# Grouped-query attention: the order of scores, turns and values on TensorE

## The chip, the cores and the metric

The kernel runs on one core of a Trainium2 chip. The metric is the device time of one execution in microseconds; before the change it is 1549.0 us, the median of 3 runs (1548.19 to 1549.32). The core has five engines that run side by side and wait for each other through semaphores: TensorE (PE in the profile, its weight loads PEld), VectorE (DVE), ScalarE (ACT), GpSimd (POOL) and SyncE (SP), which issues most transfers. Each engine works through its own instructions in one fixed order.

## The reference

One step of a two-layer trunk with 640 tokens: 512 latent tokens and 128 prompt tokens, model width 1024, 16 heads of 64. Layer 0 mixes tokens with neighbourhood attention, layer 1 with grouped-query attention, and each is followed by a gated ConvFFN. All of it is fp32. The change is in the attention of layer 1, which computes for the latent tokens

```python
qs, ks_ = axial_rope(qs), axial_rope(ks_)                 # after per-head RMS norms
k_all = jnp.concatenate([ks_, cache_gqa_k[:, i]], axis=1) # 512 latent + 128 cached keys
v_all = jnp.concatenate([vs, cache_gqa_v[:, i]], axis=1)
s = jnp.einsum('bqkgd,bskd->bkgqs', qi, k_all) * HEAD_DIM ** -0.5
p = jax.nn.softmax(s, axis=-1)
o = jnp.einsum('bkgqs,bskd->bqkgd', p, v_all)             # 16 query heads, 4 key heads
```

and then `xs + g * rmsnorm(o @ w_o)`. The prompt's own attention, 128 queries on 128 keys, is small beside it.

## The kernel before

The layers run one after the other. In layer 1 the products for keys, values and queries come first, then the attention loop, then the output projection `y` (`Mix`, L724) and the ConvFFN. The attention loop stands at L1838 and takes 34 steps.

Its work is cut into 32 **units**, `Unit` (L1663). A unit is one head and one half of the latent queries (256 of 512). Units come in the order: half 0 of heads 0 and 1, half 1 of heads 0 and 1, half 0 of heads 2 and 3, and so on. Two units that follow each other, an even and an odd one, form a **pair**. A unit goes through three stages:

- **Scores** (L1680), in two batches of 128 queries, called `s0` and `s1`. A batch is four matmuls on TensorE into a tile of two PSUM banks (`d0` for `s0`, `d1` for `s1`, one buffer each, so a batch waits until the batch before in the same tile has been read). DVE takes the minimum (L1691; the queries carry a minus sign, so it stands for the maximum), ACT the Exp with its sum (L1692), DVE the reciprocal (L1694), POOL multiplies by it (L1695).
- **Turns** (L1697). The 640 probabilities of each batch must be transposed: ten turns of 128 x 128 per unit, in three groups of 4, 4 and 2. Each group takes one PSUM bank `tp` from a list (`Banks`, L77), and ACT (L1706) or DVE (L1708) copies it to SBUF as `pk`. ACT copies the first group of every unit and the third of even units, DVE the others. The bank goes back to the end of the list; whoever gets it next waits for that copy.
- **Values** (L1713), for both units of a pair together: ten matmuls into the bank `po`. The bank is taken at half 0 and given back only after half 1 of the same two heads, when ACT casts it (L1725) and DVE subtracts (L1726).

Of the eight PSUM banks four belong to `d0` and `d1` in the loop (L1764 to L1766), and four stand in the list for `tp`, `po` and the prompt's steps.

What runs in which order is written out by hand in `GORDER` (L70): one list for even steps, one for odd ones. At step `u`, `s0` and `s1` are the scores of unit `u + 2`, `t0` to `t2` the three turn groups of unit `u`, `l0` to `l2` those of unit `u - 1`, `v` the values of the units `u - 2` and `u - 1`, and `p` one step of the prompt's attention (from step 6 on, until they are used up). TensorE runs its instructions in just that order (L110). On ACT, DVE and POOL a scheduler chooses the order when the program is built, from the same program.

At the loop's end the four banks of the scores are handed to the list (L1857), the output projection starts at step 30 with the weights `wh` and `wl`, which ACT and DVE split out of `wr` (L178, L180), and the turns of the last pair run between its products.

Of the kernel before, what the change touches and what calls it, by code (L numbers as in the profile page):

```python
# [66 lines left out]
DLEAD = 3  # L67
DPRE = (8, 10, 12, 14)
KP = (2, 2, 2, 2, 1)
GORDER = ("s0 p v s1 t0".split(), "s0 l1 l2 t0 s1 t1 t2".split())  # L70


def raw_ap(ap, offset, dims):
# [31 lines left out]
def hybrid_step(ctx: ExitStack, tc: tile.TileContext, A, O):  # L105
# [1707 lines left out]
    with ExitStack() as s:  # L1813
# [24 lines left out]
        for u in range(NU + 2):  # L1838
            if u + 2 < NU:
                un[u + 2] = Unit(u + 2)  # L1840
            for step in GORDER[u % 2]:
                if step == "p":
# [119 lines left out]
```

## Time and profile before

| what | value |
|---|---|
| median of 3 runs | 1549.0 us (1548.19 to 1549.32) |
| profiled execution, its own time | 1550.43 us |
| its span | 1548.6 us |
| granted TensorE clock, mean | 0.998 |
| busy: PE, PEld, DVE, ACT, POOL | 98%, 87%, 66%, 55%, 45% of the span |
| the attention loop | about 921 to 1063 us of the span |

The profile shows one execution. Its span runs from the first to the last instruction; the execution's own time is a little longer. A row of the timeline gives the start in us, the duration in us, engine, line of the kernel, operation, out<-in and the count of merged instructions; what stands in brackets is the idle time before and who ended it. TensorE's matmuls overlap, so their cost is read from one start to the next. The records of a product of fp32 values count two for each matmul. Names there leave buffer numbers out: `s` is a score tile, `gp` the probabilities, `nmg` the minimum, `rcg` the reciprocal, `tp`, `pk` and `po` as above, `gkh` and `gkl` the two parts of the keys, `gq` the queries.

### The profile page before, as it was taken

What the parts mean: (1) busy time and instruction counts of PE and PEld (TensorE: products, weight loads), DVE (VectorE), ACT (ScalarE), POOL (GpSimd) and SP (SyncE); (2) the same over time, 40 slices, a digit from 0 to 9 for tenths busy, and PEclk for the clock granted to TensorE, in tenths of its full rate; (3) what the DMA queues carried; (4) which work ended last, traced back from release to release, by engine and by line L of the source; (5) the groups of instructions that cost most, each with busy time, mean ns of one, the idle gap of its engine ahead of it and who ended that gap; (6) DMA issues with size and microseconds to landing.
All of it is one profiled execution on the core that took longest, in us unless ns stands there. A gap on an engine that the chain in (4) does not pass through costs nothing.

```text
span 1548.6 us, 26098 instructions
## 1 busy us (share of the span) xinstructions
PE 1513.5 (98%) x9709; PEld 1343.4 (87%) x9709; DVE 1022.3 (66%) x1648; ACT 854.0 (55%) x1624; POOL 702.2 (45%) x606
## 2 busy tenths in 40 slices
PE   6999999999999999999999999999999999999998
PEld 5988998888999999978887878778899999988886
DVE  4553343659877666755757877773988887786554
ACT  5664564646655555554544447763665665564443
POOL 1554564432355455525443464532235666542433
PEclk9999999999999999999999999999999999999999
DMA  9745454253565665388574421015433335447664
GB/s 324 199 123 161 121 134 116 64 189 125 176 225 182 222 190 162 111 279 272 174 238 153 131 67 44 2 34 196 153 115 114 120 110 158 132 161 251 226 220 131
DMA packets 196666, 243.99 MB, mean 158 GB/s; under 512 B 11484, under 2 KB 153020, under 8 KB 196540
## 3 DMA queue, kind: packets, MB, share of 16 engines
q1 hardware_dynamic: 186704, 235.74, 47.8%
q10 hardware_dynamic: 9836, 6.59, 2.5%
q8 instruction: 76, 1.25, 0.3%
q14 instruction: 50, 0.41, 0.1%
HBM read 214.38 MB, written 26.34 MB: 155 GB/s over the span
## 4 chain that ended last, share of the span: by engine, by line
PE 63%; DVE 5%; ACT 2%; issue 2%; POOL 2%; DMA 1%; POOLq 0%; DVEq 0%; ACTq 0%
PE ux L117 18%; PE acc L117 17%; PE uz L117 8%; PE gp L117 5%; PE uy L117 4%; PE po L117 3%; PE y L117 2%; PE s L117 2%; PE tp L120 2%; PE ada L117 1%; DMA wr<-in_ffn_w_down 1%; DVE t L1281 1%; POOL wl L180 1%; DMA wr<-in_ffn_w_up 1%; DVE wl L180 1%
## 5 line engine op out<-in xcount | busy, mean ns | idle before, releaser
L180 POOL TENSOR_TENSOR wl<-wr,wh 128x1024 fp32r<-128x1024 f32 x70 | 173.8, 2487 | 239.8 <-ACT wh L178 228.7
L1204 POOL TENSOR_TENSOR wl<-wr,wh 128x1024 fp32r<-128x1024 f32 x76 | 183.6, 2438 | 46.9 <-ACT wh L1203 43.3
L117 PE MATMUL ux<-B,wh 128*128 128x322 f32 x832 | 200.0, 311 | 0.9 <-ACT u L1258 0.9
L1281 DVE SCALAR_TENSOR_TENSOR t<-C,cw,t 128x644 f32<-128x644 f32 x176 | 156.4, 888 | 51.3 <-ACT t L1279 50.7
L178 ACT CAST wh<-wr 128x1024 fp32r<-128x1024 f32 x140 | 145.5, 1048 | 53.8 <-DMA wr<-in_ffn_w_down 41.1
L117 PE MATMUL acc<-wh,alo 128*128 128x512 f32 x440 | 172.3, 392 | 0.3 <-DVE alo L1173 0.3
L117 PE MATMUL acc<-wl,ahi 128*128 128x512 f32 x440 | 171.9, 391 | 0.5 <-POOL wl L180 0.5
L117 PE MATMUL acc<-wh,ahi 128*128 128x512 f32 x440 | 171.9, 391 | 0.0
L117 PE MATMUL uz<-B,wh 128*128 128x322 f32 x640 | 156.2, 312 | 0.9 <-ACT v L1258 0.9
L117 PEld LDWEIGHTS ux<-B,wh 128*128 128x128 f32 x832 | 143.6, 189 | 3.3 <-issue 1.2
L1173 DVE TENSOR_TENSOR alo<-ain,ahi 128x384 fp32r<-128x384 f32 (+1 forms) x88 | 81.8, 948 | 88.9 <-ACT ahi L1171 88.6
L117 PE MATMUL ux<-B,wl 128*128 128x322 f32 x416 | 129.5, 311 | 3.0 <-DVE wl L1204 3.0
L117 PE MATMUL qk<-hT,wh 128*128 128x384 f32 (+1 forms) x512 | 122.3, 315 | 0.0
L117 PEld LDWEIGHTS uz<-B,wh 128*128 128x128 f32 x640 | 110.9, 189 | 4.4 <-ACT v L1258 1.5
L1204 POOL TENSOR_TENSOR vl<-wr,vh 128x1024 fp32r<-128x1024 f32 x38 | 96.4, 2537 | 24.6 <-ACT vh L1203 24.3
L1203 ACT CAST wh<-wr 128x1024 fp32r<-128x1024 f32 x84 | 84.8, 1049 | 40.9 <-DVE wr L1227 40.6
L1279 ACT ACTIVATE t<-C,cw 128x644 f32<-128x644 f32 x88 | 78.6, 893 | 47.8 <-DVE C L1309 40.2
L180 DVE TENSOR_TENSOR wl<-wr,wh 128x1024 fp32r<-128x1024 f32 x70 | 91.4, 1315 | 19.3 <-ACT wh L178 18.7
L117 PE MATMUL uz<-B,wl 128*128 128x322 f32 x320 | 99.6, 311 | 0.3 <-POOL wl L1204 0.3
L117 PEld LDWEIGHTS acc<-wl,ahi 128*128 128x128 f32 x440 | 82.6, 188 | 18.9 <-POOL wl L180 0.9
L117 PEld LDWEIGHTS acc<-wh,alo 128*128 128x128 f32 x440 | 82.5, 188 | 18.7 <-DVE alo L1173 1.1
L117 PEld LDWEIGHTS acc<-wh,ahi 128*128 128x128 f32 x440 | 82.6, 188 | 17.7
(259 smaller groups left out, 3858.2 us busy)
## 6 DMA issues: line engine op xcount, KB each, us to landing
wr<-in_ffn_w_up SPq DMA_DIRECT2D x88, 512.0 KB
wr<-in_ffn_w_down SPq DMA_DIRECT2D x88, 512.0 KB
wr<-in_ada_w SPq DMA_DIRECT2D x72, 512.0 KB
act<-act SPq DMA_DIRECT2D x44, 321.0 KB
wr<-in_na_w_qkv SPq DMA_DIRECT2D x24, 512.0 KB
mod<-modrow SPq DMA_DIRECT2D x20, 512.0 KB
ain<-act SPq DMA_DIRECT2D x44, 192.0 KB
wf<-in_ada_w SPq DMA_DIRECT2D x16, 512.0 KB
```

The costliest lines, as they stand in the source:

```text
L117: pe(nc.tensor.matmul(*a, **k))
L120: pe(nc.tensor.transpose(*a, **k))
L178: i = nc.scalar.copy(hi, raw)
L180: j = (low or nc.vector).tensor_sub(lo, raw, f32(hi))
L1173: pin(nc.vector.tensor_sub(lo[:, 0 : c1 - c0], ain[:, 0 : c1 - c0], f32(hi[:, 0 : c1 - c0])))
L1203: nc.scalar.copy(hl[0], src)
L1204: low.tensor_sub(hl[1], src, f32(hl[0]))
L1279: nc.scalar.activation(t, taps(0), AF.Identity, bias=cw[:, 3, n : n + 1], scale=cw[:, 1, n : n + 1])
L1281: nc.vector.scalar_tensor_tensor(t, taps(d), cw[:, w, n : n + 1], t, op0=ALU.mult, op1=ALU.add)
```

## The change

The two lists are written anew. The diff is complete:

```diff
-GORDER = ("s0 p v s1 t0".split(), "s0 l1 l2 t0 s1 t1 t2".split())
+GORDER = ("s0 p v s1".split(), "s0 l0 l1 l2 t0 t1 t2 s1".split())
```

Even steps lose their turn group. Odd steps do all six groups of the pair, even unit first, between `s0` and `s1`. An even step's `s1` is now followed at once by the odd step's `s0`, and an odd step's `s1` by the even step's `s0`. Line numbers stay as they are.

The first place is TensorE in one pair in the middle of the loop, from the values of one pair to those of the next. Before:

```order
L117 MATMUL po<-pk,gvt 64x256 x10
L117 MATMUL s_11455<-gkh,gq_9265 128x320 x2
L117 MATMUL s_11455<-gkl,gq_9265 128x320 x2
L120 MATMUL tp<-ident,gp 128x128 x4
L117 MATMUL s_11475<-gkh,gq_9266 128x320 x2
L117 MATMUL s_11475<-gkl,gq_9266 128x320 x2
L120 MATMUL tp<-ident,gp 128x128 x10
L117 MATMUL s_11503<-gkh,gq_9266 128x320 x2
L117 MATMUL s_11503<-gkl,gq_9266 128x320 x2
L120 MATMUL tp<-ident,gp 128x128 x6
L117 MATMUL s_11528<-gkh,gq_9265 128x320 x2
L117 MATMUL s_11528<-gkl,gq_9265 128x320 x2
```

Now:

```order
L117 MATMUL po<-pk,gvt 64x256 x10
L117 MATMUL s_11455<-gkh,gq_9265 128x320 x2
L117 MATMUL s_11455<-gkl,gq_9265 128x320 x2
L117 MATMUL s_11468<-gkh,gq_9266 128x320 x2
L117 MATMUL s_11468<-gkl,gq_9266 128x320 x2
L120 MATMUL tp<-ident,gp 128x128 x20
L117 MATMUL s_11515<-gkh,gq_9266 128x320 x2
L117 MATMUL s_11515<-gkl,gq_9266 128x320 x2
L117 MATMUL s_11528<-gkh,gq_9265 128x320 x2
L117 MATMUL s_11528<-gkl,gq_9265 128x320 x2
L117 MATMUL po<-pk,gvt 64x256 x10
```

Twenty turns that stood in three pieces between four score batches now stand in one; the score batches stand two by two.

The second place is ACT in the same pair. `gp_11431` is the Exp of the even unit's batches (its second reads `s2_11455`), `pk_...<-tp_...` are the copies of turn groups. Before:

```order
L1692 ACTIVATE gp_11431,sug_11433<-s2_11435,nmg_11432 128x640
L1706 COPY pk_11469<-tp_11464 128x512
L1692 ACTIVATE gp_11431,sug_11433<-s2_11455,nmg_11432 128x640
L1706 COPY pk_11494<-tp_11491 128x256
L1692 ACTIVATE gp_11471,sug_11473<-s2_11475,nmg_11472 128x640
L1706 COPY pk_11501<-tp_11496 128x512
L1692 ACTIVATE gp_11471,sug_11473<-s2_11503,nmg_11472 128x640
```

Now:

```order
L1692 ACTIVATE gp_11431,sug_11433<-s2_11435,nmg_11432 128x640
L1692 ACTIVATE gp_11431,sug_11433<-s2_11455,nmg_11432 128x640
L1706 COPY pk_11482<-tp_11477 128x512
L1692 ACTIVATE gp_11464,sug_11466<-s2_11468,nmg_11465 128x640
L1706 COPY pk_11494<-tp_11491 128x256
L1706 COPY pk_11501<-tp_11496 128x512
L1692 ACTIVATE gp_11464,sug_11466<-s2_11515,nmg_11465 128x640
```

The copy of the pair's first turn group stood ahead of the Exp of `s2_11455` and now stands behind it; the next two copies stand behind the Exp of the batch after it. In this pair the bank `po` is held; in the pairs in which it has just been cast, the first copy stands ahead of both Exps.

The third place is TensorE at the loop's end, where the output projection begins. Before:

```order
L117 MATMUL s_11788<-gkh,gq_9266 128x320 x2
L117 MATMUL s_11788<-gkl,gq_9266 128x320 x2
L120 MATMUL tp<-ident,gp 128x128 x6
L117 MATMUL po<-pk,gvt 64x256 x10
L120 MATMUL tp<-ident,gp 128x128 x4
L117 MATMUL y_11855<-wh,ph_10242 128x512
L117 MATMUL y_11855<-wl,ph_10242 128x512
```

Now:

```order
L117 MATMUL s_11800<-gkh,gq_9266 128x320 x2
L117 MATMUL s_11800<-gkl,gq_9266 128x320 x2
L117 MATMUL po<-pk,gvt 64x256 x10
L117 MATMUL y_11848<-wh,ph_10242 128x512
L117 MATMUL y_11848<-wl,ph_10242 128x512
L117 MATMUL y_11848<-wh,pl_10243 128x512
```

The last scores now stand directly ahead of the values, and the four turns behind the values have moved behind the first `y` group, where sixteen turns of before have become twenty.

## The prediction

> **What bounds the kernel now.** I read the page first, then the stage of the grouped-query scores by windows, then TensorE's timeline in it. The page's first row is TensorE's; the row below it is the loop that the change edits, 924 to 1040 us.
>
> ```profile
> PE 1513.5 (98%) x9709; PEld 1343.4 (87%) x9709; DVE 1022.3 (66%) x1648; ACT 854.0 (55%) x1624; POOL 702.2 (45%) x606
> ```
> ```profile
> 924.00:1040.00 116.00, 113.23 (x875) 92.06 (x876) 86.93 (x184) 85.01 (x201) 54.51 (x72) 1.00 0.06 19
> ```
>
> In the loop the columns are the length, then busy time of PE, PEld, DVE, ACT and POOL, the clock and the DMA share. TensorE is never long idle, ACT has 85 of 116 us and DVE 87, POOL and DMA little. So TensorE's order of work sets the pace, and what it waits for is ACT and DVE handing back PSUM. One pair of units, from value product to value product, on TensorE (start, duration, engine, line):
>
> ```profile
> 1007.20 2.38 PE L117 MATMUL po<-pk,gvt 128*64 128x256 f32 x20
> 1009.51 0.56 PE L117 MATMUL s<-gkh,gq 128*128 128x320 f32 x2
> 1009.91 0.46 PE L117 MATMUL s<-gkl,gq 128*128 128x320 f32 x2
> 1010.21 0.60 PE L120 MATMUL tp<-ident,gp 128*128 128x128 f32 x4
> 1010.56 0.54 PE L117 MATMUL s<-gkh,gq 128*128 128x320 f32 x2
> 1010.94 0.46 PE L117 MATMUL s<-gkl,gq 128*128 128x320 f32 x2
> 1011.23 1.25 PE L120 MATMUL tp<-ident,gp 128*128 128x128 f32 x10
> 1012.27 0.56 PE L117 MATMUL s<-gkh,gq 128*128 128x320 f32 x2
> 1012.67 0.46 PE L117 MATMUL s<-gkl,gq 128*128 128x320 f32 x2
> 1013.08 0.87 PE L120 MATMUL tp<-ident,gp 128*128 128x128 f32 x6
> 1013.71 0.53 PE L117 MATMUL s<-gkh,gq 128*128 128x320 f32 x2
> 1014.08 0.45 PE L117 MATMUL s<-gkl,gq 128*128 128x320 f32 x2
> 1014.46 2.38 PE L117 MATMUL po<-pk,gvt 128*64 128x256 f32 x20
> ```
>
> Costs go from start to start. The values take 2.31; a score batch 0.70 after values, 0.67 after turns (1010.56 to 1011.23), 0.75 between turns and values; ten turns 1.04, so 0.105 each. The pair takes 7.26, of which 0.2 is waiting: the batch at 1012.27 holds on for 0.81 instead of 0.67, and six turns take 0.63.
>
> There are 14 such intervals between the first value product at 928.45 and the one at 1036.00. I split them by whether the burst of turns inside runs while `po` keeps a PSUM bank (half 0 of a head pair has been summed, half 1 not: 7 intervals, "held") or after `po` was copied out (7, "freed"). These windows show the sum of the held ones; of the freed ones a plain one, the last, and the sum.
>
> ```profile
> sum 51.49, PE 51.49; mean PE 7.36
> ```
> ```profile
> 1014.46:1022.16 7.70, 7.42 (x57) 1.00 0.01 2
> 1029.42:1036.00 6.58, 6.58 (x53) 1.00 0.00 1
> sum 56.06, PE 54.07; mean PE 7.72
> ```
>
> A held interval without a prompt step is 7.26, as above; five of the freed ones carry a prompt step and are longer.
>
> **What the change takes away and adds on TensorE.** Nothing is removed: per pair it stays at 16 score matmuls, 20 turns, 10 value products. Only the order differs, so the work alone is 2.31 + (0.70 + 0.59) + 20 x 0.105 + (0.67 + 0.67) = 7.04. The 0.59 is a batch behind another: four times half of the 0.29 that two matmuls take from 1010.94 to 1011.23. Before it is 7.26 - 0.2 = 7.06. Grouping the kinds buys 0.02 per pair, nothing.
>
> What the old order pays is the score tile's reuse: d0 and d1 each wait until the Exp before has read them.
>
> ```profile
> PEld s L117 <- ACT gp L1692: 6.9, 13, 1.2
> PE s L117 <- ACT gp L1692: 2.9, 7, 0.9
> ```
>
> The shortest distance there is d1, between the two batches at 1009.51 and 1012.27; the new order spaces both tiles by either values plus a batch (2.9) or the burst plus a batch (2.7). From the end of a batch to the end of its Exp I need 0.82 + 0.8 + 0.2 (rows below), about 1.9, so these waits go.
>
> **What it adds: the banks.** A burst of 20 turns is six fills of a bank: even unit 4, 4, 2, then odd unit 4, 4, 2. Four banks are in the list, three when `po` holds one. So in a held burst fill 4 needs the bank of fill 1, and 6 that of 3, both copied out by ACT. The order of ACT's rows shows that in held pairs the Exp of the first side-by-side batch is queued ahead of that first copy, and the Exp of the second ahead of the third fill's copy. ACT and DVE durations:
>
> ```profile
> 1006.93 0.80 ACT L1692 ACTIVATE gp<-s,nmg 128x640 f32<-128x640 f32 x1 [0.27 <-DVE nmg L1691]
> 1010.84 0.59 ACT L1706 COPY pk<-tp 128x512 f32<-128x512 f32 x1 [1.11 <-PE tp L120]
> 1011.33 0.81 ACT L1692 ACTIVATE gp<-s,nmg 128x640 f32<-128x640 f32 x1
> 1012.11 0.37 ACT L1706 COPY pk<-tp 128x256 f32<-128x256 f32 x1
> 1016.91 0.59 ACT L1725 CAST ph<-po 128x512 fp32r<-128x512 f32 x1
> ```
> ```profile
> 1006.07 0.82 DVE L1691 TENSOR_REDUCE nmg<-s 128x1 f32<-128x640 f32 x1 [0.46 <-PE s L117]
> 1010.41 0.82 DVE L1691 TENSOR_REDUCE nmg<-s 128x1 f32<-128x640 f32 x1 [0.48 <-PE s L117]
> 1012.33 0.69 DVE L1708 COPY pk<-tp 128x512 f32<-128x512 f32 x1
> 1013.16 0.82 DVE L1691 TENSOR_REDUCE nmg<-s 128x1 f32<-128x640 f32 x1
> 1013.90 0.15 DVE L1694 RECIPROCAL rcg<-sug 128x1 f32<-128x1 f32 x1
> 1018.41 0.68 DVE L1726 TENSOR_TENSOR pl<-po,ph 128x512 fp32r<-128x512 f32 x1
> ```
>
> A minimum starts 0.04 after the scores' end (1009.91 + 0.46 to 1010.41) and takes 0.82, though DVE goes on after 0.74 (1013.16 to 1013.90); the Exp starts 0.04 after that (1006.89 to 1006.93) and gives ACT free after 0.78 (1011.33 to 1012.11); a copy of 512 columns takes 0.59 and ACT goes on after 0.49. A bank comes back to TensorE about 0.05 after its copy (1012.33 + 0.69 to 1013.08).
>
> A held pair, from the end of the values: first batch 0 to 0.70, visible at 0.86; minimum 0.90 to 1.72; Exp 1.76, ACT free at 2.54; first copy 2.54 to 3.13; fill 4 may start at 3.18. TensorE is there at 0.70 + 0.59 + 10 x 0.105 = 2.34: it waits **0.84**. Fills 4 and 5 then end at 4.02. ACT meanwhile: second Exp 3.03 to 3.81, third copy to 4.18, so fill 6 may start at 4.23: **0.21** more. The pair is 7.04 + 1.05 = 8.09, against 7.26: +0.83. The values at 5.78 wait for nothing: fill 5's last turn is through at about 4.02 + 0.25 (the four-turn row's 0.60 less its 0.35), its copy on DVE 0.69 later, about 5.0. Seven of them: **+5.8**.
>
> A freed pair: ACT casts `po` 0.14 after the values (1016.91 less 1016.77) to 0.73, DVE subtracts from 0.77 (0.68, of which I let the next overlap 0.08 as behind the minimum), runs two minima at 0.74 each and reaches the copy of fill 2 at 2.85, done 3.54. Fill 6 needs that bank: 3.59 against 3.18, a wait of 0.41, so 7.45 where the trace has 7.70: -0.25. That holds for the one plain interval. The five with a prompt step have another bank or more ACT work ahead of the burst; the ends are -0.25 and the held pair's +0.83, and I take +0.2 each, nearer the freed row. Together **+0.7**. The last interval has one batch less: 2.31 + 1.29 + 2.10 + 0.41 + 0.75 = 6.86 against 6.58, **+0.3**.
>
> **The two ends of the loop.** At the start four turns stood in a wait and cost nothing:
>
> ```profile
> 923.20 0.60 PE L120 MATMUL tp<-ident,gp 128*128 128x128 f32 x4
> 924.74 0.56 PE L117 MATMUL s<-gkh,gq 128*128 128x320 f32 x2 [0.94 <-ACT gp L1692]
> ```
>
> They move behind that batch: **+0.4** (from 0 to 0.8, if a bank is late too). At the end, the output projection's first matmuls wait for their weights, which ACT splits only after the last Exp:
>
> ```profile
> 1036.00 2.64 PE L117 MATMUL po<-pk,gvt 128*64 128x256 f32 x20
> 1038.57 0.66 PE L120 MATMUL tp<-ident,gp 128*128 128x128 f32 x4
> 1039.50 0.50 PE L117 MATMUL y<-wl,ph 128*128 128x512 f32 x1
> ```
> ```profile
> 1037.10 3.88 ACT L178 CAST wh<-wr 128x1024 fp32r<-128x1024 f32 x4
> ```
> ```profile
> 1038.16 4.69 DVE L180 TENSOR_TENSOR wl<-wr,wh 128x1024 fp32r<-128x1024 f32 x4 [0.68 <-ACT wh L178]
> ```
>
> From these values to the first `y<-wl` it is 3.50. Between the last scores and the values stood six turns (0.63 in the pair above); in the new order the scores stand directly before the values, so 3.50 becomes 4.13: +0.63, and up to 1.1 as the last minimum queues behind two copies on DVE; I take 0.9. The four turns at 1038.57, free today, move into the later burst between the `y` groups: 0.4. Together **+1.3**. From there everything is released by these matmuls; loads of later weights start when their buffers are read, so they shift along and cover nothing.
>
> Sum: 5.8 + 0.7 + 0.3 + 0.4 + 1.3 = **+8.5 us**. The profiled run has a span of 1548.6 (1550.4 with what lies around it), 0.4 and 1.4 us from the runs' median of 1549.0, on which I put it: **1557.5 us**. Bounds: with fill 6 never late in held pairs (+0.62), freed ones all at -0.25 and the last at 0, no loss at the start and 0.6 at the end it is +3.4; with held pairs at +1.1 (the Exp 0.27 later), prompt intervals at +0.83, and 0.8, 0.5 and 2.0 for start, last interval and end, about +15.
>
> **Rivals.** *The score waits were the real price (faster).* If ACT gets to each first copy before fill 4 asks for it, held pairs fall to 7.04 (51.49 - 49.3 = 2.2 saved), six freed ones lose 0.66 each (4.0), and the ends cost 1.7: 1544.5. For it stand the 9.8 us of waits above; against it, ACT's order in held pairs. It decides where the wait at the fourth fill is under 0.2.
>
> *A wash.* If `po`'s bank does not matter, held bursts wait 0.41 like freed ones: 7.45, +0.19 each, 1.3; freed ones at -0.25 take 1.5 back, the last gives 0.3: with both ends of the loop covered 1549. Against it: the list has four banks, and a value product keeps one until half 1.
>
> *Later copies hold up the values too.* Fill 5's copy stands behind two reciprocals on DVE that wait for the Exps. If it lands 0.5 after the values are due in each of 14 intervals, 7 us come on top: 1564.5. My layout leaves 0.7 of slack.
>
> *The clock falls in the bursts.* At half clock 16 bursts of 2.10 take 34 us more: 1591. The trace has a burst of sixteen turns at the loop's end, and it ran at the full granted clock:
>
> ```profile
> 1048.90:1050.57 1.67, 1.67 (x18) 1.00 1.02 410
> ```
>
> The Trainium skill ("TensorE: Matmul & The Clock Gate", Part 4: PE-mode transpose) says that transposes do not count as busy for the clock gate, and by that rule longer bursts could let the clock drop. The row just shown does not agree; a repeated burst of twenty no run here shows yet.
>
> That the change doesn't do what it says is out: the order shows twenty turns in one row.
>
> **How the numbers follow.** Forecast 0.83, wash 0.06, faster 0.04, late values 0.06, clock 0.01. A measurement here tells about 0.2% (3.1 us) from no change. Faster is the first rival, 0.04; same is most of the wash, 0.05; slower 0.91. The range 1553.5 to 1561 runs from near the lower bound to half-way between forecast and upper bound and leaves about 2 in 10 out.
>
> **What would show it.** Right: held intervals near 8.1, with a wait of TensorE's turns on ACT's copy (L1706) of some 0.8; freed ones near 7.4 without a prompt step; waits of scores on the Exp nearly gone; 1.00 clock; `y<-wl` some 4.4 after the last values but one start. Wrong: if held intervals stay at 7.3 the bank argument falls; if the value products wait for copies, the late-values rival holds.

## The result, and the profile after

The change takes 1557.58 us, the median of 4 runs (1556.74 to 1558.56). The kernel before took 1549.09 us beside it (4 runs, 1548.19 to 1549.32). The ratio is 1.0056, with a 95% interval of 1.0044 to 1.0068: slower by 8.5 us, and by more than the 0.2% that a measurement here can tell. The profiled execution took 1557.03 us, with a span of 1554.9.

The first row of the page after:

```profile
PE 1513.8 (97%) x9709; PEld 1344.1 (86%) x9709; DVE 1026.3 (66%) x1648; ACT 850.8 (55%) x1624; POOL 702.0 (45%) x606
```

TensorE has the same work in the same number of instructions. The span is longer by what it waits. The windows of the loop after, TensorE alone, split as in the prediction: the sum of the seven held intervals, the sum of the seven freed ones, and one plain interval of each kind (from:to, length, busy time of PE with its count, granted clock, DMA share, GB/s).

```profile
sum 57.45, PE 52.54; mean PE 7.51
sum 55.44, PE 53.92; mean PE 7.70
1009.82:1017.88 8.06, 7.33 (x57) 1.00 0.00 0
1017.88:1025.36 7.48, 7.31 (x57) 1.00 0.00 0
```

The held intervals grew from 51.49 to 57.45. The freed ones did not grow: 55.44 against 56.06. Before, TensorE was busy for all of the held 51.49; now 4.9 of the 57.45 are idle.

Three rows of the view of waits after (us in total, times, longest):

```profile
PE tp L120 <- ACT pk L1706: 4.6, 7, 0.7
PE tp L120 <- DVE pk L1708: 1.8, 8, 0.5
PEld s L117 <- ACT gp L1692: 3.8, 10, 0.4
```

The row in which TensorE's score matmuls waited for the Exp (2.9 us before) has no successor, and the loads' wait on it fell from 6.9 to 3.8. New are the first two rows. Seven times a turn waits for ACT's copy, once in each held interval. Eight times one waits for DVE's copy: at the sixth fill of each freed interval, and once in the held one at 943.33, which carries other work. TensorE in one held pair, from the values of one pair to those of the next:

```profile
1025.36 2.38 PE L117 MATMUL po<-pk,gvt 128*64 128x256 f32 x20
1027.67 0.56 PE L117 MATMUL s<-gkh,gq 128*128 128x320 f32 x2
...
1028.65 0.46 PE L117 MATMUL s<-gkl,gq 128*128 128x320 f32 x2
1028.94 1.25 PE L120 MATMUL tp<-ident,gp 128*128 128x128 f32 x10
1030.93 1.40 PE L120 MATMUL tp<-ident,gp 128*128 128x128 f32 x10 [0.73 <-ACT pk L1706]
1032.08 0.54 PE L117 MATMUL s<-gkh,gq 128*128 128x320 f32 x2
...
1033.03 0.46 PE L117 MATMUL s<-gkl,gq 128*128 128x320 f32 x2
1033.42 0.87 PE L117 MATMUL po<-pk,gvt 128*64 128x256 f32 x6
```

The loop's first burst, which waits for nothing:

```profile
923.90 2.35 PE L120 MATMUL tp<-ident,gp 128*128 128x128 f32 x20
926.00 0.54 PE L117 MATMUL s<-gkh,gq 128*128 128x320 f32 x2
```

Twenty turns take 2.10 there (923.90 to 926.00). In the held pair they take 3.14 (1028.94 to 1032.08), so 1.04 of it is waiting. The burst stops after ten turns, that is, after fills 1 to 3. Inside a burst of this trace one turn starts 0.109 after the one before, so ten turns with more behind them take 1.09; from 1028.94 to 1030.93 it is 1.99. The fourth fill waits 0.90 and the second ten turns lose the other 0.14. ACT at that place:

```profile
1029.42 0.80 ACT L1692 ACTIVATE gp<-s,nmg 128x640 f32<-128x640 f32 x1 [1.66 <-DVE nmg L1691]
1030.21 0.58 ACT L1706 COPY pk<-tp 128x512 f32<-128x512 f32 x1
1030.67 0.81 ACT L1692 ACTIVATE gp<-s,nmg 128x640 f32<-128x640 f32 x1
```

The copy of fill 1 runs from 1030.21 to 1030.79, right behind the first Exp, and the fourth fill starts 0.14 after its end. The loop's last values and the first products of the output projection:

```profile
1040.24 2.72 PE L117 MATMUL po<-pk,gvt 128*64 128x256 f32 x20
...
1044.75 0.49 PE L117 MATMUL y<-wl,ph 128*128 128x512 f32 x1 [0.76 <-DVE wl L180]
```

From the values to the first `y<-wl` it is 4.51 (3.50 before).

The whole loop, from its first score matmul to its last value product, by starts:

| part of the loop (us) | before | after | difference |
|---|---|---|---|
| first score to first values | 7.05 | 7.46 | +0.41 |
| seven held intervals | 51.49 | 57.45 | +5.96 |
| five freed intervals with a prompt step | 41.78 | 41.14 | -0.64 |
| the plain freed interval | 7.70 | 7.48 | -0.22 |
| the last freed interval | 6.58 | 6.82 | +0.24 |
| values of the last pair but one to those of the last | 24.31 | 25.79 | +1.48 |
| sum | 138.91 | 146.14 | +7.23 |

### The profile page after: what moved, and what is told of

Read it like the earlier page. It is cut to its first block, busy times and chain, and to the rows that moved or that the text cites. A ratio compares the mean times of both kernels' runs of the same rounds, so it can differ in the third digit from the quotient of the medians.

```text
span 1554.9 us, 26071 instructions
## 1 busy us (share of the span) xinstructions
PE 1513.8 (97%) x9709; PEld 1344.1 (86%) x9709; DVE 1026.3 (66%) x1648; ACT 850.8 (55%) x1624; POOL 702.0 (45%) x606
## 4 chain that ended last, share of the span: by engine, by line
PE 59%; DVE 7%; issue 3%; ACT 3%; DMA 3%; POOL 2%; ACTq 0%; POOLq 0%; DVEq 0%
PE ux L117 18%; PE acc L117 15%; PE uz L117 8%; PE uy L117 4%; PE gp L117 3%; PE y L117 2%; PE po L117 2%; PE s L117 2%; PE tp L120 2%; PE ada L117 1%; DMA wr<-in_ffn_w_down 1%; DVE nmg L1691 1%; POOL wl L180 1%; DMA wr<-in_ffn_w_up 1%; DVE wl L180 1%
```

## The experiments

Two readings of the loss in held bursts stood against each other. By the first, the *order on ACT* is the cause: an Exp stands ahead of the first copy. By the second, the *number of banks* is: six fills with three banks need ACT and DVE to hand back three of them within the burst, whatever stands first. Beside them the score tiles' reuse and the two ends of the loop were priced. Each kernel was profiled; where a ratio is given, it is against the kernel before, run beside it on the same chip. Medians of before there were 1549.0 us (first four experiments, 18 runs), 1548.1 (next four, 18 runs) and 1548.64 (last four, 15 runs).

### The bank of the values given back after every pair

```diff
 # values
-        if u.hf == 0:
-            ta["po"] = bk.get("po")
+        ta["po"] = bk.get("po")
...
+        c, src = slice(256 * u.hf, 256 * u.hf + 256), ta["po"][:, 256 * u.hf : 256 * u.hf + 256]
+        nc.scalar.copy(hi[:, c], src)
+        nc.vector.tensor_sub(lo[:, c], src, f32(hi[:, c]))
+        bk.put(ta["po"])
```

ACT's cast and DVE's subtraction of 512 columns behind every second pair become 256 columns behind every pair, and every burst has four banks.

> The changed kernel, but the value products of each pair get a bank of their own and give it back at once (ACT casts and DVE subtracts 256 columns per pair instead of 512 per two pairs), so that no burst of turns runs with three banks. Bank theory: held intervals fall from 8.06 to 7.5 to 7.6 (the burst then waits only for fill 2's copy on DVE, as in the freed intervals, 7.48), the rest stays; seven held intervals give 7 x -0.5 = -3 to -4, the extra cast and subtraction take some of it back: about 1554.5 us, 0.997 to 0.999 of the changed kernel. Rival 'the number of banks does not matter, score batches side by side are slow as such': held intervals stay at 8.06 and the time at 1557.6. Rival 'later copies hold the values': no change either.

Measured: 1550.38 us (10 runs), ratio 1.0011 [1.0001, 1.0020]. The sums of held and freed intervals in the windows of this kernel, named by their places although no burst has a bank too few any more; then a plain held one and the plain freed one:

```profile
sum 52.59, PE 51.56; mean PE 7.37
sum 54.05, PE 53.26; mean PE 7.61
1007.75:1015.20 7.45, 7.25 (x57) 1.00 0.00 0
1015.20:1022.40 7.20, 7.20 (x57) 1.00 0.00 0
```

The bank takes back 4.9 of the 6.0 us that the held intervals had lost, and 1.4 come off the freed ones: the median falls by 7.2, from 1557.58. The plain held intervals are 7.20 to 7.46 (8.06 in the change), the plain freed one 7.20 (7.48).

The scheduler also chose a new order on ACT, and that has to be kept apart from the bank. In the held interval of 7.45 and in the next one ACT has the order of the change: Exp (from 1011.81), first copy (from 1012.59), the other Exp. There the fourth bank alone turns 8.06 into 7.45, although ACT and DVE also have 256 columns of `po` to read that the change does not read there; only the fifth fill still waits, 0.4, for the copy of fill 1. In the intervals of 7.20, such as the freed one shown, the first copy stands ahead of both Exps (1019.42, 1019.91, 1020.69), and no turn waits. Between the freed 7.20 and the 7.48 of the change lie this order of ACT and half as many columns of `po` to cast and subtract; the two were not tried apart.

### One bank less

```diff
         mod_row()
+        held = bk.get("held")
...
+            if u == NU - 3:
+                bk.put(held)
```

> The changed kernel with one bank of the list set aside during the loop: two instead of three banks in held bursts, three instead of four in freed ones. Bank theory: freed plain interval from 7.48 to about 8.0, as held ones are with three banks; held ones from 8.06 to about 8.5; about 14 x 0.45 = +6 us, 1564 us. Rival 'banks do not matter': 1557.6, intervals unchanged.

Measured: 1565.44 us (4 runs), ratio 1.0105 [1.0090, 1.0120]. A plain held and a plain freed interval:

```profile
1015.01:1023.63 8.62, 7.59 (x58) 1.00 0.00 0
1023.63:1031.49 7.86, 7.45 (x58) 1.00 0.01 2
```

ACT keeps the order of the change in both. With that order plain held pairs take 8.62 with two banks, 8.06 with three (the change) and 7.45 with four (the kernel above); plain freed ones 7.86 with three and 7.48 with four. So the number of banks sets the length of the burst, and in this order one bank is worth 0.4 to 0.6 us a pair.

### ACT's first copy ahead of the second Exp

```diff
-                    un[u + 2].scores(int(step[1]))
+                    if u % 4 == 2 and step == "s1":
+                        wait_exp = un[u + 2].scores(1, True)
+                    else:
+                        un[u + 2].scores(int(step[1]))
...
+                    if step == "l0" and wait_exp:
+                        wait_exp(un[u - 1].ci)
```

In held pairs the Exp of the even step's `s1`, which ran ahead of the first copy, is put behind it: with `True`, `scores` hands back its Exp, reciprocal and multiplication to be issued later, and `ci` is the copy of `l0`.

> The changed kernel with ACT's queue turned round in held pairs: the Exp of the first side-by-side batch goes behind the copy of the burst's first fill. Theory A (the prediction's wording: that Exp ahead of the first copy costs 0.84 at fill 4): that wait goes, held intervals fall from 8.06 to about 7.4, 7 x -0.65 = -4.5 us, 1553 us. Theory B (what sets the burst is all that ACT must do before the third fill's copy, two Exps and the first copy, whatever their order): fill 4 starts 0.5 sooner and fill 6 then waits that much longer; held intervals stay at 8.1 to 8.2, 1557.5 to 1558.5 us.

Measured: 1558.62 us (4 runs), ratio 1.0065 [1.0050, 1.0080]: not better than the change. The plain held interval in the windows:

```profile
1011.40:1019.62 8.22, 7.49 (x57) 1.00 0.00 0
```

TensorE's burst in one held pair, and ACT beside it:

```profile
1030.68 2.48 PE L120 MATMUL tp<-ident,gp 128*128 128x128 f32 x18
1033.78 0.44 PE L120 MATMUL tp<-ident,gp 128*128 128x128 f32 x2 [0.62 <-ACT pk L1714]
```
```profile
1031.32 0.59 ACT L1714 COPY pk<-tp 128x512 f32<-128x512 f32 x1 [1.82 <-PE tp L120]
1031.80 0.80 ACT L1694 ACTIVATE gp<-s,nmg 128x640 f32<-128x640 f32 x1
1032.58 0.79 ACT L1694 ACTIVATE gp<-s,nmg 128x640 f32<-128x640 f32 x1
1033.35 0.86 ACT L1714 COPY pk<-tp 128x256 f32<-128x256 f32 x2
```

Eighteen turns stand in one row now. The row is 2.48 long, where eighteen turns without a wait take 2.13 (at 1037.01 in the change): the fourth fill still waits 0.3 for the copy of fill 1, which ends at 1031.91, instead of 0.90. But the copy of fill 3 now stands behind both Exps, and the sixth fill waits 0.8 for it. The whole burst takes 3.29 (1030.68 to the scores at 1033.97), so 1.19 of it is waiting, against 1.04 in the change. Most of the wait has moved from fill 4 to fill 6, and it has grown. With three banks, the order of Exp and first copy alone is not the cause. With four it matters: the first experiment has 7.20 with the copy ahead and 7.45 with the Exp ahead.

### First and third copy together

```diff
 # as the kernel above, and in turns:
-            if j == 0 or j == 2 and self.b == 0:
+            if j == 0 or j == 2 and self.b == 1:
```

The copy of fill 3 goes to DVE, that of fill 6 to ACT.

> As the run with ACT's queue turned round, and the third fill's copy (256 columns, even unit) goes to DVE, the sixth fill's to ACT instead. Theory B: now neither fill 4 nor fill 6 waits for the Exps; fill 4 from about 2.4 to 2.6 after the values, fill 6 at about 3.45 for DVE's copy, so held intervals about 7.3 (7 x -0.75 = -5), freed ones +0.1 each for the extra DVE copy: about 1552.5 us. Theory A: the same as the run with the copy first, since fill 4 was all. If neither bank nor copies matter: 1557.6.

Measured: 1553.39 us (9 runs), ratio 1.0031 [1.0021, 1.0041]. The plain held interval:

```profile
1006.97:1014.36 7.39, 7.28 (x58) 1.00 0.00 0
```

Now three banks nearly do: 7.39. What is left is a wait of 0.3 at the fourth fill, for the copy of fill 1. The plain freed interval, where DVE also has the subtraction of `po`, is 7.69 instead of 7.48, twice the loss that was expected.

### The third copy alone

The one line of the kernel above, on the change.

> The changed kernel with the third fill's copy on DVE and the sixth's on ACT, the Exp left ahead of the first copy in held pairs. Theory B (fill 4 waits until 3.2 for the first copy, fill 6 then asks at about 4.0 and finds its bank copied at 3.4): only the second of the two waits goes, held intervals 7.75 to 7.9 instead of 8.06, plain freed ones about 7.7; 1556 to 1557 us. If the third copy were all that counts, held intervals would be 7.4, as with both edits.

Measured: 1556.09 us (one run). The plain held interval:

```profile
1009.89:1017.84 7.95, 7.22 (x57) 1.00 0.00 0
```

This completes a square of held intervals: neither edit 8.06, first copy early 8.22, third copy on DVE 7.95, both 7.39. Alone, the edits bring -0.16 and 0.11; together 0.67. Plain held intervals of one execution differ by 0.02 at most in these four kernels. So there is no single late copy: two fills of the burst, the fourth and the sixth, wait for ACT, and to free one lets TensorE run into the other.

### One score batch back in the burst

```diff
-GORDER = ("s0 p v s1".split(), "s0 l0 l1 l2 t0 t1 t2 s1".split())
+GORDER = ("s0 p v s1".split(), "s0 l0 l1 l2 s1 t0 t1 t2".split())
```

> The changed kernel with the odd step's last score batch put into the middle of the burst, ten turns ahead of it and ten behind. Bank theory: ACT and DVE get a batch's time (0.67) more between fill 3 and fill 4, so the turns' waits on copies go; but the batch now comes 1.6 behind the batch before it in the same score tile and waits for its Exp: 0.3 in held intervals (7.4), about 1.0 in freed ones, where that Exp stands behind the first copy (plain one 8.1). Together about 1554.5 to 1555.5. Rival 'score batches side by side are slow as such': held and freed both fall to about 7.3.

Measured: 1555.30 us (4 runs), ratio 1.0047 [1.0033, 1.0061]. Sums of held and freed intervals:

```profile
sum 53.19, PE 52.08; mean PE 7.44
sum 59.61, PE 53.96; mean PE 7.71
```

Held intervals recover 4.3 us: the batch gives the copies 0.7 us more in the middle of the burst, and in the view of waits no turn waits for a copy any more. But freed ones lose 4.2 us, to this wait on TensorE in a freed pair:

```profile
1022.50 1.25 PE L120 MATMUL tp<-ident,gp 128*128 128x128 f32 x10
1024.57 0.56 PE L117 MATMUL s<-gkh,gq 128*128 128x320 f32 x2 [0.81 <-ACT gp L1692]
```

The batch after ten turns comes before the Exp has read its tile: 2.07 from start to start, 1.03 more than ten turns take. This is the price of a score tile that is asked for again too early; the prediction said that the change removes it, and the change does.

### The old lists at the end of the loop

```diff
-            for step in GORDER[u % 2]:
+            for step in (GORDER if u < NU - 4 else GOLD)[u % 2]:
```

`GOLD` holds the two lists of before.

> The changed kernel, with the old lists for the loop's last four units and its end alone. The prediction's end term: from the last values to the first y<-wl back from 4.51 to 3.5 (here six turns stand between the last scores and the values again), and the four turns stand in that wait again: last value product to last value product 25.79 to about 24.3; 1.4 us in all. If the end term were something else (the weights' transfer, the banks handed over), these distances would stay.

Measured: 1558.28 us (one run), no better than the change in total. TensorE at the loop's end (the lines are one further down here):

```profile
1042.32 2.50 PE L118 MATMUL po<-pk,gvt 128*64 128x256 f32 x20
...
1045.77 0.50 PE L118 MATMUL y<-wl,ph 128*128 128x512 f32 x1
```

From the values to `y<-wl` it is 3.45, and the last part of the loop takes 24.29 where the change has 25.79: the end term is 1.5 us, and it comes from the order of the last steps. The total hides it, since in this execution the loop's start took 9.07 instead of 7.46, at a lower clock (last section).

### Both cures, with the new lists and with the old

Two kernels take the bank given back after every pair and the third copy on DVE: one with the new lists and the old end, one with the old lists throughout.

> New lists with the bank of the values given back after every pair, the third fill's copy on DVE and the sixth's on ACT, and the old lists at the loop's end. Theory B: no burst with three banks, no third copy behind two Exps: held 7.1 to 7.2 without a prompt step, freed plain 7.1, end as before: about 1546.5 us, 2 to 3 us under the kernel before. If only the order of the lists decided, it would stay near 1556.

> The kernel before with its old lists, and the same two edits of banks and copies: the bank of the values given back after every pair, third fill's copy on DVE, sixth's on ACT. Theory B: the gain of those two is not the new order's own; intervals near 7.2, freed plain 7.2 instead of 7.70, about 1546 us, the same as the new lists with these edits. If the new order is worth something once the banks are free, this one is slower than the new lists with the edits by 1 us or more.

Measured beside each other: new lists 1546.56 us (11 runs), ratio 0.9994 [0.9986, 1.0003]; old lists **1543.94 us** (8 runs), ratio 0.9973 [0.9962, 0.9984]. Sums of held and freed intervals, new lists and then old lists:

```profile
sum 51.92, PE 51.49; mean PE 7.36
sum 53.73, PE 53.30; mean PE 7.61
```
```profile
sum 50.79, PE 50.79; mean PE 7.26
sum 52.46, PE 52.46; mean PE 7.49
```

With the old lists TensorE does not idle in any interval, and a plain one is 7.09; with the new lists it is 7.20. So the new order gains nothing even when its banks are there: it costs 2.6 us more in the medians and 2.8 in the loop (137.34 against 134.53), against the expectation that the two would come out the same or the new lists ahead. Of the 2.4 us between the intervals, 1.2 lie in two that carry other work (944.80 and 953.03), in each of which a turn of the new lists still waits 0.4 for a copy of DVE. The rest is about 0.1 a pair. Where that comes from shows in the waits of weight loads between 935 and 1030, new lists and then old lists:

```profile
PEld s L118 <- ACT gp L1693: 5.7, 21, 0.4
```
```profile
PEld s L117 <- ACT gp L1692: 2.1, 6, 0.4
```

and in the two batches ahead of the values, with the new lists:

```profile
1013.17 0.54 PE L118 MATMUL s<-gkh,gq 128*128 128x320 f32 x2
1013.55 0.45 PE L118 MATMUL s<-gkl,gq 128*128 128x320 f32 x2
1013.91 0.56 PE L118 MATMUL s<-gkh,gq 128*128 128x320 f32 x2
1014.31 0.45 PE L118 MATMUL s<-gkl,gq 128*128 128x320 f32 x2
1014.69 1.08 PE L118 MATMUL po<-pk,gvt 128*64 128x256 f32 x8
```

They take 1.52 here, against 1.34 in the change (1032.08 to 1033.42): the second batch starts 0.07 late and its first step takes 0.40 instead of 0.29. In a pair of 8.06 the score tiles were free in time; in one of 7.20 the second is asked for before its Exp is through.

### The bank alone with the old lists

The old lists with the edit of the first experiment and nothing else.

> The kernel before with its old lists and the bank of the values given back after every pair, alone. Bank theory: the old order too waits for banks and for the cast and subtraction of 512 columns in freed intervals; plain freed one from 7.70 to about 7.2, held without a prompt step as before (7.2 to 7.3), about -1.7 us: 1546.5 to 1547.5 us. If the gain of both edits in the old lists (0.9973) came from the copies' assignment alone, this one stays at the kernel before.

Measured: 1546.32 us (11 runs), ratio 0.9986 [0.9977, 0.9995], loop 136.14. The held intervals come to 51.89 and the freed ones to 52.97. So of what the best kernel saves in the loop against before (138.91 to 134.53, 4.4 us), 2.8 come with this edit and 1.6 with the third copy. But the 2.8 are not the price of a held bank. Plain held intervals fall from 7.26 to 7.09, yet three that carry other work grow (to 8.04, 7.97 and 7.54), and the seven together are 0.4 longer than before. The gain lies in the freed ones, 3.1 us, where `po` kept no bank before either. There the kernel before had six waits of scores for the Exp (2.0 us between 935 and 1030), and in three of them its chain of work that ended last runs from the cast of 512 columns over the subtraction and a minimum to that Exp (from 970.53, 986.55 and 1002.17). Now a single freed interval has such a wait. That fits the halved cast and subtraction, which no run tries alone. The old order paid little for the bank itself.

### The two kernels once more

> The changed kernel once more, for the loop's start: in some executions of the new order the profile shows a slot of 3.4 us at half the granted clock at the first burst. If the new order brings it about, it shows here in about one of two or three executions: first scores of the loop to first value product 7.46 without it, 9.1 with it.

> The kernel before once more, for the same: if the slot belongs to the new order, the clock stays at 1.00 at the loop's start and first scores to first value product take 7.05; if it comes by chance in either order, it may show here too (about 8.6).

Measured: the change 1558.33 us (span 1556.2), before 1549.73 (span 1547.9), one run each. Neither shows the slot: from the first scores to the first values it is 7.45 and 7.04. The loop is 146.11 and 138.91, within 0.03 of the first executions. The spans differ by 8.3 here and by 6.3 in the first two executions, so what lies outside the loop moves by about a microsecond in either direction from one execution to the next; the loop here does not.

## Why the prediction was right, and where its steps were not

**The total.** Forecast 1557.5, measured 1557.58. That is closer than its steps deserve: they sum to +8.5, and the loop as measured lost 7.23. The other 1.3 us between the medians lie outside the loop, where the traces show no step of the change. From one execution to the next that part moves by as much, so its place is not settled. That the total fits to 0.1 is luck: two misses, the freed intervals below and this part, cancel.

**Held intervals.** The sum said 8.09 with 1.05 of waiting, 0.84 at the fourth fill and 0.21 at the sixth. Measured: 8.06 with 1.04, of which 0.90 at the fourth fill. Its layout holds step by step, counted from the end of the values (1027.67): the minimum starts at 0.89 (forecast 0.90), the Exp at 1.75 (1.76), the first copy at 2.54 (2.54), the fourth fill at 3.26 (3.18), 0.14 after the copy instead of 0.05. All seven wait, +5.96 against +5.8.

**Its cause.** The prediction named the bank that `po` keeps, and within the burst the Exp ahead of ACT's first copy. The bank is shown: with the same order on ACT, two, three and four banks give 8.62, 8.06 and 7.45. The Exp is where the wait ends, but its place is not what the wait costs: with the copy ahead of that Exp the interval was 8.22. The fourth and the sixth fill both hang on ACT. The 0.84 and 0.21 add up for the queue as it stands, but the 0.84 can't be had back alone: once the fourth fill was earlier, the sixth waited 0.8.

**Freed intervals, the mis-sized term.** Plain one 7.48 (forecast 7.45), last one 6.82 (6.86). The five with a prompt step were put at +0.2 each, between the ends -0.25 and +0.83; they measured -0.64 together, -0.13 each. Three of them did not change at all (-0.01 each), and two got shorter, as the plain one did (-0.22 and -0.39). None moved towards the held pair's +0.83, and the wait is the forecast one: the sixth fill, for DVE's copy, in each of the seven. This is the one term that was off by more than 0.3, 1.6 us in all, and by chance what lies outside the loop made up for it.

**The score waits.** "These waits go" holds for the score matmuls of the change (from the first burst on none waits for the Exp any more) and in part for their weight loads (3.8 us of 6.9 stay, all ahead of the first batch after the values, which starts 2.31 after them with that wait or without). It does not hold as a property of the order: at 7.20 a pair the loads wait again, 5.7 us in 95. And "grouping the kinds buys nothing" was still kind to it: without bank waits the new order is 0.11 a plain pair dearer than the old one (7.20 against 7.09, where the working had 7.04 and 7.06).

**The ends.** Start +0.41 (forecast +0.4). `y<-wl` 4.51 after the values (4.4), the whole end +1.48 (+1.3); with the old lists for the last steps it is back at the old value.

**The rivals.** Faster and the wash fell at the mark that they had set, a wait under 0.2 (or 7.45) in held bursts. Late values did not show: from the last score matmul to the value product it is 0.39 (1033.03 to 1033.42), as for a batch without a wait. The clock in the repeated bursts, in the windows after (all engines):

```profile
935.00:1030.00 95.00, 90.17 (x698) 72.48 (x696) 68.16 (x145) 62.77 (x157) 41.73 (x54) 1.00 0.04 12
```

A dozen bursts of twenty turns, 8 us apart, ran at the full granted clock, so the clock rival fell. (A fall of the clock at the loop's start, for another reason, is told in the last section.) The rule that transposes do not count as busy (the Trainium skill, "TensorE: Matmul & The Clock Gate", Part 4: PE-mode transpose) is not borne out by this row, nor by the stretches at the end of the last section, in which TensorE did next to nothing but turns and kept the full clock.

## What to carry to other kernels

Before the order of work on the tensor engine is changed, count the fills of PSUM that will stand in a row against the banks that are free at that moment, with every accumulator that keeps one; where fills outnumber banks, price all copies that must come back within the burst together, since curing one alone (8.22 or 7.95 for 8.06 here) may only move the wait to the next. An accumulator that is read out in halves and gives its bank back at once gained in both orders here, 7.2 us with the new lists and 2.3 with the old ones, and 1543.9 us was reached with the old lists and a copy moved to the other engine as well. A wait that vanishes when a loop gets slower has not been removed; look for it again when the loop is fast.

## What was not expected

At the loop's first burst the clock fell in some executions. Two stretches of the kernel with the old end, in its windows (TensorE alone):

```profile
921.00:923.40 2.40, 0.98 (x5) 1.00 0.01 2
923.40:926.80 3.40, 3.20 (x14) 0.53 0.00 1
```

In the change TensorE is as little busy in the first stretch, 1.02 us, and the second ran at 1.00. Here the second ran at about half the clock: the first twenty turns took 3.18 from start to start instead of 2.10, the batch before them 1.23 instead of 0.68, and the start of the loop 9.07 instead of 7.46. Of ten profiled executions with the new lists three had such a slot (bank given back, batch in the burst, old end), of four with the old lists none. The Trainium skill ("TensorE: Matmul & The Clock Gate", Part 1: The HAM clock gate) gives the gate a free-running window of 3.4 us. The traces agree. The slots are 3.413 us long, and in every trace the records of the granted clock change at distances that are whole multiples of this: 264 of them, 901.119 us, lie between the end of a slot at 19.10 us and the start of this one at 923.63. So the clock is set on a grid of 3.413 us, and from one execution to the next the grid lies elsewhere on the program.

Laid on that grid, the fourteen traces tell when a slot comes. They hold 6262 steps of the grid between the first and the last change of the clock on record. The twelve steps that are followed by a slot have 1.02 to 1.81 us of TensorE's work in them; the 6250 others have 1.81 or more. (The ends of matmuls are modelled in these traces, so the limit is a rough figure. Nine of the twelve slots stand elsewhere, eight of them before 23 us, in kernels with either lists.) In the three executions with a slot at the first burst, the step ahead of it has 1.80 or 1.81, from 920.22 to 923.63 with the old end; in the seven others with the new lists the emptiest step there has 1.97 to 2.57.

That settles whose slot it is. Wherever the grid were to lie, a step at the loop's start would have at least 2.22 with the old lists (921.34 to 924.75 in the kernel before), too much for a slot. With the new lists it can have as little as 1.78 (919.82 to 923.23 in the change), and at 0.28 of all places of the grid it has 1.81 or less; three of ten executions had the slot. The four turns that the old lists do between these scores fill part of that stretch. This is a cost of the change that the sum of the prediction doesn't have: some 1.6 us, in about every fourth execution by the traces' grid.

The turns themselves count as work on this grid. With one bank less, the step from 1035.52 to 1038.93 has 2.38 us of work, of which 0.17 are scores and the rest turns, and the clock stayed at 1.00 behind it. Without its turns that step would be far below the 1.02 that was followed by a slot.
